# The first matrix of a single expert's block loaded and split amid the pair's block before it; the last pair block left whole

## The chip, the cores and the metric

The kernel runs on one core of one Trainium2 chip. The metric is device time in microseconds; before the change the median of three runs is 1378.51 us (1378.15 to 1379.26). The engines are PE (TensorE, matmuls), ACT (ScalarE), DVE (VectorE), POOL (GpSimd) and SP (SyncE, which issues nearly all loads here).

## The reference, cut to what matters

A decoder trunk of two layers over 256 positions of width 1024. The second layer ends in a mixture of experts: eight SwiGLU networks of hidden width 3584, of which each position uses two. What the change touches is this part alone:

```python
logits = (x2d @ router).astype(F32)
top_val, top_exp = lax.top_k(logits, TOP_K)          # 2 of 8
gates = jax.nn.softmax(top_val, axis=-1)
...
def expert_block(args):
    xb, e = args
    return (jax.nn.silu(xb @ w1[e]) * (xb @ w3[e])) @ w2[e]
```

All weights are fp32 and lie in HBM; the eight experts are 352 MB.

## The kernel before, in words

The kernel sorts the experts by how many positions chose them. The four fullest have room for 128 positions each and are computed one at a time, as **single** experts; the other four have room for 64 and are computed two at a time, as **pairs**: on PE the two experts of a pair use the two halves of the array's columns.

An expert's hidden width is cut into blocks of 512 columns, seven to an expert. A block is: the product with w1 (`up` or `up2`), silu of it on ACT (line 700), the product with w3, the gate product of both on DVE (line 711), four transposes of that (`gate_T`, lines 625 and 632), a copy or split of the transposed tile, and the product with w2 (`down`). The down products of a block are issued inside the following block, behind its w1 and silu. The blocks stand in a list `items` in the order single, single, pair; this **cycle** comes 14 times. In the kernel before, the last pair's last block is cut into two of 256 columns, so one more pair block follows at the end. At an expert's first block, `pre` gathers that expert's positions (lines 976 and 1001), and the down products of the block before are woven into that; in one block it first tests whether an expert has more positions than room (`overflow`, a branch that all engines take; line 888).

Single experts use a split: each weight tile comes from HBM as fp32 and is turned into hi (ACT, line 222, rounded to fp32r) and lo (DVE, line 223, what is left). `mm3` then makes three fp32r matmuls for each tile (lines 232 to 234). A block's w1 is two loads of 1 MB (`pieces`), four splits (p1 to p4) and 24 matmuls. The hi and lo tiles have five buffers each. Pair experts use fp32 directly: no split, four loads of 1 MB for each matrix (two halves of the rows, two experts), and 16 matmuls for each, which the trace records as two each (line 285 in `up2`, line 651 in `down`), so 32.

All these loads go through SP's queue in the order of the code, into 11 tiles of 1 MB in rotation; a load waits until the tile eleven loads before it has been read. In a cycle these are 24 loads.

The order of the instructions on each engine is not written out: the Tile framework plans it when the program is built. Its planner goes through the program with its own estimate of durations and gives each engine, of the instructions that it then holds ready, the one that stands first in the code. On the chip each engine keeps that order. So an instruction may be planned ahead of an earlier one that the planner believed to be waiting, and it stays there even where the chip would have had the earlier one ready.

In `swiglu` a block runs so: `step(u, 2)` issues the first half of w1's products, then `gate_T` of the block before, then `end(u)` the rest, then silu, `down` of the block before, then w3. In the list's last block (`held`) the down of the block before comes behind w3 instead. `tail=sums` starts the final sums (line 874) between the last down products.

Of the kernel before, what the change touches and what calls it, by code (L numbers as in the profile page):

```python
# [28 lines left out]
D_FFE = 3584  # L29
# [123 lines left out]
def trunk(ctx: ExitStack, tc: tile.TileContext, a, out, R=6, WB=5, NF=16):  # L153
# [60 lines left out]
    def load(w, r0, nr, c0, ncol):  # L214
        t = raw()
        v = t[:, :nr * ncol].rearrange("p (k f) -> p k f", k=nr)
        src = w.at(r0, nr, c0, ncol)
        nc.sync.dma_start(v if len(src.shape) == 3 else t[:, :nr * ncol], src)
        return v
# [16 lines left out]
    def pieces(w, c0, ncol, n, m=4):  # L236

        for r in range(0, KT, m):
            v = load(w, r, m, c0, ncol)
            for q in range(0, m, n):  # L240
                yield (r + q, *split(v[:, q:q + n, :]))
# [19 lines left out]
            sh, sl = s(k + j)  # L261
            mm3(o[:, :n], sh, sl, wh[:, j, :], wl[:, j, :], k + j == 0, k + j == KT - 1)

    def up(outs, w, c0, ncol, sta, ws=None, between=None):


        if ws is None:
            for q in pieces(w, c0, ncol, 2):
                for o, s in zip(outs, sta):
                    products(o, s, *q)  # L270
                yield
        else:
            for i in range(len(sta)):
                for q in ws:
                    products(outs[i], sta[i], *q)
                if i == 0 and between:
                    between()

    def up2(o, ws, c0, ncol, sta):

        for r in (0, 4):
            vs = [load(w, r, 4, c0, ncol) for w in ws]
            for k in range(4):
                for i, v in enumerate(vs):
                    TE.matmul(o[i * 64:(i + 1) * 64, :ncol], lhsT=sta(r + k, i), rhs=v[:, k, :], start=r + k == 0,  # L285
                              stop=r + k == KT - 1)
                if k % 2:
                    yield
# [175 lines left out]
    sta = halves(xTh, xTl)  # L464
# [126 lines left out]
    w1, w3, w2 = W["even_w1"][0], W["even_w3"][0], W["even_w2"][0]  # L591
# [9 lines left out]
    ws = ahead(w1, *chunks[0])  # L601
# [14 lines left out]
    def swiglu(items, ws, between=None, behind=None, next_ws=None, tail=None):  # L616

        def gate_T(it, g):  # L620
            n = it[4]
            if isinstance(it[0], tuple):
                pt, t = wk(), fa("gt")
                for j in range(n // P):
                    TE.transpose(pt[:, j * P:(j + 1) * P], g[0][:, j * P:(j + 1) * P], ident)
                A.copy(t[:, :n], pt[:, :n])  # L626
                return t
            gs = []
            for q in g:
                pt = wk()  # L630
                for j in range(n // P):
                    TE.transpose(pt[:, j * P:(j + 1) * P], q[:, j * P:(j + 1) * P], ident)  # L632
                gh, gl = fb("gh"), fb("gl")
                A.activation(gh[:, :n], pt[:, :n], AF.Copy)
                V.tensor_sub(gl[:, :n], pt[:, :n], gh[:, :n].bitcast(F32))  # L635
                gs.append((gh, gl))
            return gs

        def down(it, gs, fill=iter(())):
            w1, w3, w2, c0, n, sta, accs, first, last, pre, post = it  # L640
            nr = n // P
            accs = accs()
            if isinstance(w1, tuple):
                m = 1 if tail and it is items[-1] else 2
                for r in range(0, nr, m):
                    ws = [load(w, c0 // P + r, m, 0, D) for w in w2]
                    for j in range(m):
                        for d in range(2):
                            for i, w in enumerate(ws):
                                s = slice((r + j) * P + i * 64, (r + j) * P + (i + 1) * 64)  # L650
                                TE.matmul(accs[0][d][i * 64:(i + 1) * 64, :], lhsT=gs[:, s],  # L651
                                          rhs=w[:, j, d * 512:(d + 1) * 512], start=first and r + j == 0,
                                          stop=last and r + j == nr - 1)
                            step(fill)
                end(fill)
                if post:
                    post()
                return
            for r in range(0, nr, 2) if not last else [0]:
                ws = []  # L660
                m = 1 if tail and it is items[-1] else 2
                for q in range(r, nr if last else r + 2, m):
                    v = load(w2, c0 // P + q, m, 0, D)
                    ws += [split(v[:, j:j + 1, :]) for j in range(m)]
                for i, (gh, gl) in enumerate(gs):
                    for d in range(2):
                        for j, (wh, wl) in enumerate(ws):
                            s = slice((r + j) * P, (r + j + 1) * P)
                            c = slice(d * 512, (d + 1) * 512)
                            mm3(accs[i][d], gh[:, s], gl[:, s], wh[:, 0, c], wl[:, 0, c],  # L670
                                first and r + j == 0, last and r + j == nr - 1)
                            step(fill)
            end(fill)
            if post:
                post()

        prev = after = None
        for it in items:
            if it is items[-1] and next_ws:
                after = next_ws()  # L680
            w1, w3, w2, c0, n, sta, accs, first, last, pre, post = it
            fill = pre() if pre else None
            if fill:
                if prev:
                    step(fill, 3)
                    down(prev[0], gate_T(*prev), fill)
                    prev = None
                else:
                    end(fill)
            sta = sta()  # L690
            p1 = [wk() for _ in sta]
            two = isinstance(w1, tuple)
            u = up2(p1[0], w1, c0, n, sta[0]) if two else up(p1, w1, c0, n, sta, ws, between)
            step(u, 2)
            if prev:
                gs = gate_T(*prev)
            end(u)
            s = [fa("sl") for _ in sta]
            for q, p in zip(s, p1):
                A.activation(q[:, :n], p[:, :n], AF.Silu)  # L700
            held = tail and it is items[-1]
            if prev and not held:
                down(prev[0], gs)
            p3 = [wk() for _ in sta]
            with tc.issue_after(behind) if ws else nullcontext():
                end(up2(p3[0], w3, c0, n, sta[0]) if two else up(p3, w3, c0, n, sta))
            ws = None
            if held:
                down(prev[0], gs)
            for q, p in zip(s, p3):  # L710
                V.tensor_mul(q[:, :n], q[:, :n], p[:, :n])  # L711
            prev = (it, s)
        down(prev[0], gate_T(*prev), *([tail()] if tail else []))
        return after and after + next_ws(4)
# [5 lines left out]
    ws = swiglu([(w1, w3, w2, c0, n, lambda: sta, lambda: accs, i == 0, i == len(chunks) - 1, None, None)  # L720
            for i, (c0, n) in enumerate(chunks)], ws, rest, behind, lambda r=0: ahead(odd_in, 0, 512, r))
# [18 lines left out]
    p1 = proj(1)  # L740
# [4 lines left out]
    w1, w3, w2 = (W[q] for q in ("odd_w1", "odd_w3", "odd_w2"))  # L745
    ws = ahead(w1[0], 0, 512)
# [81 lines left out]
    with tc.issue_after(behind):  # L828
# [13 lines left out]
        for h in range(2):  # L842
# [8 lines left out]
            q = cp.tile([P, 8], F32, name=nm("slots"))  # L851
# [222 lines left out]
    def expert(q):  # L1074
        end_ = q == 6
        ch = [(c, 512) for c in range(0, D_FFE, 512)]
        if end_:
            ch[-1:] = [(D_FFE - 512, 256), (D_FFE - 256, 256)]
        ws3 = list(zip(picked(q), picked(q + 1))) if CAP[q] == 64 else picked(q)
        for i, (c, n) in enumerate(ch):  # L1080
            first, last = i == 0, i == len(ch) - 1
            pre = None
            if first:
                pre = lambda: begin([q])
            elif (q, i) == (0, 1):
                pre = residual
            elif (q, i) == (2, 2):
                pre = overflow
            yield (*ws3, c, n, lambda: state["sta", q], lambda: e_acc(q), first, last, pre,
                   (lambda: combine(q, end_)) if last else None)  # L1090

    alone, paired = run(*(expert(q) for q in range(4))), run(expert(4), expert(6))
    items = []
    for it in alone:
        items += [it, next(alone), next(paired)]
    items += paired
    swiglu(items, ws, behind=behind, tail=sums)


# [53 lines left out]
```

## Time and profile before

| | us |
|---|---|
| median of three runs | 1378.51 |
| lowest, highest | 1378.15, 1379.26 |
| the profiled execution | 1374.65 |
| its span, first to last instruction | 1372.9 |
| mean granted clock of TensorE | 0.982 |

| engine | busy, us | share |
|---|---|---|
| PE | 1301.1 | 95% |
| DVE | 784.9 | 57% |
| ACT | 614.4 | 45% |
| POOL | 53.7 | 4% |

The expert stage begins at about 460 us of the span and lasts to its end. Times in rows are microseconds from the start of the span. Matmuls are pipelined and the profiler models their ends, so a row of PE can overlap the next one by up to some tenths of a microsecond; starts are exact.

### The profile page before, as it was taken

Reading aid. Unit: us, or ns where it says so; the run is one execution under the profiler, and the core shown is the slowest. Engines: PE = TensorE matmul, PEld = TensorE weight load, DVE = VectorE, ACT = ScalarE, POOL = GpSimd, SP = SyncE. Lnnn points to the kernel's source line nnn. Section 1 sums busy time; section 2 is a strip of 40 time slices with the busy share of each in tenths; the row PEclk is TensorE's granted clock in tenths of the full one; section 3 lists DMA queues with packets and bytes.
Section 4 is the critical chain, followed back from the end, with each engine's and each line's share of the span. In section 5 each row is a group of like instructions: output and inputs, shape, how many; then the busy total and the mean of one; then the engine's idle time right before and its main releaser. Section 6 shows DMA issues by size and latency. Waiting matters only on the chain. (4 is left out here: it accounts for less than half of the span.)

```text
span 1372.9 us, 16689 instructions
## 1 busy us (share of the span) xinstructions
PE 1301.1 (95%) x6130; PEld 887.7 (65%) x6130; DVE 784.9 (57%) x1201; ACT 614.4 (45%) x859; POOL 53.7 (4%) x40
## 2 busy tenths in 40 slices
PE   8998999999999899999999999999899999999996
PEld 7776888887777775564746556466456475646562
DVE  6988445557777574463645455464446473644463
ACT  5564434443555364453444445254345353544441
POOL 0012000101021100000000000000000000000001
PEclk9999999999999699999999999999999999999998
DMA  9522456554444489999999999996999998999964
GB/s 371 193 101 103 166 184 218 221 194 162 155 151 176 170 308 396 422 420 421 412 375 421 419 420 409 381 362 226 420 421 412 405 411 344 421 415 418 394 234 167
DMA packets 69195, 426.26 MB, mean 310 GB/s; under 512 B 7920, under 2 KB 16368, under 8 KB 19824
## 3 DMA queue, kind: packets, MB, share of 16 engines
q1 hardware_dynamic: 68096, 421.70, 77.6%
q0 software_dynamic: 864, 3.15, 0.7%
q8 instruction: 50, 0.82, 0.2%
q14 instruction: 41, 0.34, 0.1%
q10 hardware_dynamic: 144, 0.26, 0.1%
HBM read 424.03 MB, written 1.05 MB: 310 GB/s over the span
## 5 line engine op out<-in xcount | busy, mean ns | idle before, releaser
L223 DVE TENSOR_TENSOR lo<-raw,hi 128x1024 fp32r<-128x1024 f32 (+1 forms) x454 | 535.2, 1220 | 244.1 <-ACT hi L222 237.3
L222 ACT ACTIVATE hi<-raw 128x1024 fp32r<-128x1024 f32 (+2 forms) x472 | 467.1, 1034 | 230.9 <-PE wk L234 124.2
L285 PE MATMUL wk<-raw,xg 128*64 128x512 f32 (+1 forms) x960 | 210.3, 568 | 0.2
L232 PE MATMUL wk<-hi,xg 128*128 128x512 f32 x448 | 179.3, 401 | 7.1 <-DVEq L888 6.6
L233 PE MATMUL wk<-lo,xg 128*128 128x512 f32 x448 | 178.4, 398 | 5.0 <-DVE lo L223 5.0
L234 PE MATMUL wk<-hi,xg 128*128 128x512 f32 x448 | 175.6, 392 | 0.0
L711 DVE TENSOR_TENSOR sl<-sl,wk 128x512 f32<-128x512 f32 (+1 forms) x55 | 36.4, 667 | 220.4 <-PE wk L285 132.4
L285 PEld LDWEIGHTS wk<-raw,xg 128*64 128x64 f32 x960 | 68.1, 137 | 120.9 <-issue 113.8
L232 PE MATMUL acc<-hi,gh 128*128 128x512 f32 x312 | 119.1, 401 | 15.1 <-ACT hi L222 14.5
L233 PE MATMUL acc<-lo,gh 128*128 128x512 f32 x312 | 123.3, 397 | 4.8 <-DVE lo L223 4.8
L234 PE MATMUL acc<-hi,gl 128*128 128x512 f32 x312 | 122.1, 394 | 1.4 <-DVE gl L635 1.2
L232 PEld LDWEIGHTS wk<-hi,xg 128*128 128x128 f32 x448 | 84.8, 189 | 43.9 <-issue 26.1
L233 PEld LDWEIGHTS wk<-lo,xg 128*128 128x128 f32 x448 | 84.9, 189 | 26.1 <-DVE lo L223 8.8
L651 PE MATMUL acc<-raw,gt 128*64 128x512 f32 x448 | 100.9, 598 | 0.3 <-ACT gt L626 0.3
L234 PEld LDWEIGHTS wk<-hi,xg 128*128 128x128 f32 x448 | 84.8, 189 | 17.0
L700 ACT ACTIVATE sl<-wk 128x512 f32<-128x512 f32 (+1 forms) x55 | 32.0, 582 | 137.1 <-PE wk L285 74.3
L232 PEld LDWEIGHTS acc<-hi,gh 128*128 128x128 f32 x312 | 58.3, 189 | 36.6 <-ACT hi L222 22.0
L233 PEld LDWEIGHTS acc<-lo,gh 128*128 128x128 f32 x312 | 59.1, 189 | 21.7 <-DVE lo L223 9.4
L232 PE MATMUL wk<-hi,xT 128*128 128x512 f32 (+1 forms) x192 | 72.6, 378 | 0.3 <-ACT xT L315 0.3
L233 PE MATMUL wk<-lo,xT 128*128 128x512 f32 (+1 forms) x192 | 71.7, 374 | 0.0
L234 PE MATMUL wk<-hi,xT 128*128 128x512 f32 (+1 forms) x192 | 71.6, 374 | 0.0
L651 PEld LDWEIGHTS acc<-raw,gt 128*64 128x64 f32 x448 | 35.2, 136 | 54.7 <-issue 54.0
(208 smaller groups left out, 1361.6 us busy)
## 6 DMA issues: line engine op xcount, KB each, us to landing
raw<-in_odd_w SPq DMA_DIRECT2D x326, 1024.0 KB, 9.7
raw<-in_even_w SPq DMA_DIRECT2D x31, 1024.0 KB, 4.8
raw<-in_odd_w_in SPq DMA_DIRECT2D x12, 1024.0 KB, 4.8
raw<-in_odd_w SPq DMA_DIRECT2D x20, 512.0 KB, 6.9
raw<-in_even_w_in SPq DMA_DIRECT2D x8, 1024.0 KB, 11.8
raw<-in_even_w_out SPq DMA_DIRECT2D x4, 1024.0 KB, 5.2
raw<-in_odd_w_out SPq DMA_DIRECT2D x4, 1024.0 KB, 5.5
raw<-in_even_w SPq DMA_DIRECT2D x4, 512.0 KB, 3.2
```

Of the source, the lines that this page charges most:

```text
L222: A.activation(hi, v, AF.Copy)
L223: by.tensor_sub(lo, v, hi.bitcast(F32))
L232: TE.matmul(o, lhsT=sh, rhs=wh, start=first, stop=False)
L233: TE.matmul(o, lhsT=sh, rhs=wl, start=False, stop=False)
L234: TE.matmul(o, lhsT=sl, rhs=wh, start=False, stop=last)
L285: TE.matmul(o[i * 64:(i + 1) * 64, :ncol], lhsT=sta(r + k, i), rhs=v[:, k, :], start=r + k == 0, stop=r + k == KT - 1)
L651: TE.matmul(accs[0][d][i * 64:(i + 1) * 64, :], lhsT=gs[:, s], rhs=w[:, j, d * 512:(d + 1) * 512], start=first and r + j == 0, stop=last a ...
L700: A.activation(q[:, :n], p[:, :n], AF.Silu)
L711: V.tensor_mul(q[:, :n], q[:, :n], p[:, :n])
```

## The change

`swiglu` now looks one block ahead. In a pair's block that is followed by a single expert's, it loads and splits the whole w1 of that next block (`list(pieces(...))`) behind the pair's down products and ahead of the pair's w3. The next block's `up` then takes these splits (`early`) instead of loading; its matmuls stay where they are in the code. And the last pair's last block is no longer cut in two, so it is the one that is `held`, and the load sizes of its down products change to two rows, one row, one row.

```diff
-    def up(outs, w, c0, ncol, sta, ws=None, between=None):
+    def up(outs, w, c0, ncol, sta, ws=None, between=None, early=None):
         if ws is None:
-            for q in pieces(w, c0, ncol, 2):
+            for q in early or pieces(w, c0, ncol, 2):
                 for o, s in zip(outs, sta):
                     products(o, s, *q)
                 yield
...
-                m = 1 if tail and it is items[-1] else 2
-                for r in range(0, nr, m):
+                for r, m in ((0, 2), (2, 1), (3, 1)) if tail and it is items[-1] else ((0, 2), (2, 2)):
                     ws = [load(w, c0 // P + r, m, 0, D) for w in w2]
...
-        prev = after = None
-        for it in items:
+        prev = after = early = None
+        for it, following in zip(items, items[1:] + [None]):
...
-            u = up2(p1[0], w1, c0, n, sta[0]) if two else up(p1, w1, c0, n, sta, ws, between)
+            u = up2(p1[0], w1, c0, n, sta[0]) if two else up(p1, w1, c0, n, sta, ws, between, early)
+            early = None
...
             if prev and not held:
                 down(prev[0], gs)
+            if two and following and not isinstance(following[0], tuple):
+                early = list(pieces(following[0], *following[3:5], 2))
             p3 = [wk() for _ in sta]
...
         ch = [(c, 512) for c in range(0, D_FFE, 512)]
-        if end_:
-            ch[-1:] = [(D_FFE - 512, 256), (D_FFE - 256, 256)]
...
     for it in alone:
         items += [it, next(alone), next(paired)]
-    items += paired
```

## Rows read from the trace of the kernel before

**Rows 1.** The page: busy us, share, count of PE; then DMA and GB/s by slice
```profile
PE 1301.1 (95%) x6130; PEld 887.7 (65%) x6130; DVE 784.9 (57%) x1201; ACT 614.4 (45%) x859; POOL 53.7 (4%) x40
...
DMA  9522456554444489999999999996999998999964
GB/s 371 193 101 103 166 184 218 221 194 162 155 151 176 170 308 396 422 420 421 412 375 421 419 420 409 381 362 226 420 421 412 405 411 344 421 415 418 394 234 167
```
**Rows 2.** Windows, one cycle: length, busy us by engine, clock, DMA share, GB/s
```profile
1008.82:1069.78 60.96, 57.94 (x253) 35.14 (x252) 30.97 (x29) 26.66 (x30) 0.00 (x0) 1.00 1.01 416
```
**Rows 3.** Timeline of PE, a pair's block: start, length, instructions, [idle before, releaser]
```profile
1258.22 1.07 PE L285 MATMUL wk<-raw,xg 128*64 128x512 f32 x2
1259.23 0.66 PE L632 MATMUL wk<-cst,sl 128*128 128x128 f32 x4
1259.81 7.08 PE L285 MATMUL wk<-raw,xg 128*64 128x512 f32 x30
1268.53 0.73 PE L232 MATMUL acc<-hi,gh 128*128 128x512 f32 x2 [1.63 <-ACT hi L222]
...
1275.04 7.09 PE L285 MATMUL wk<-raw,xg 128*64 128x512 f32 x32
...
1282.94 0.66 PE L625 MATMUL wk<-cst,sl 128*128 128x128 f32 x4 [0.38 <-DVE sl L711]
1284.08 0.50 PE L233 MATMUL wk<-lo,xg 128*128 128x512 f32 x1 [0.48 <-DVE lo L223]
...
1289.52 1.07 PE L651 MATMUL acc<-raw,gt 128*64 128x512 f32 x3
```
**Rows 4.** Timelines of DVE and ACT, the same stretch
```profile
1268.51 4.63 DVE L223 TENSOR_TENSOR lo<-raw,hi 128x1024 fp32r<-128x1024 f32 x4 [7.26 <-ACT hi L222]
1282.20 0.69 DVE L711 TENSOR_TENSOR sl<-sl,wk 128x512 f32<-128x512 f32 x1 [9.06 <-PE wk L285]
...
1267.42 5.79 ACT L222 ACTIVATE hi<-raw 128x1024 fp32r<-128x1024 f32 x6
```
**Rows 5.** Timeline of PE, the second pair's block
```profile
560.53 3.65 PE L285 MATMUL wk<-raw,xg 128*64 128x512 f32 x16
...
573.95 7.09 PE L285 MATMUL wk<-raw,xg 128*64 128x512 f32 x32
...
587.11 1.09 PE L651 MATMUL acc<-raw,gt 128*64 128x512 f32 x4
```
**Rows 6.** Waits from 520 us on: us in total, times, longest
```profile
PE acc L232 <- ACT hi L222: 14.5, 9, 1.6
...
PE wk L625 <- DVE sl L711: 4.1, 10, 0.6
```
**Rows 7.** Timeline of PE, the first of the two half blocks
```profile
1316.72 0.65 PE L285 MATMUL wk<-raw,xg 128*64 128x256 f32 x2
...
1322.48 1.95 PE L285 MATMUL wk<-raw,xg 128*64 128x256 f32 x16
```
**Rows 8.** Timeline of PE, a pair's w3 at a switch of experts
```profile
889.60 3.65 PE L285 MATMUL wk<-raw,xg 128*64 128x512 f32 x14
...
895.36 1.08 PE L651 MATMUL acc<-raw,gt 128*64 128x512 f32 x4 [0.28 <-ACT gt L626]
```
**Rows 9.** Timelines of PE and DVE behind the overflow test
```profile
970.75 0.77 PE L232 MATMUL wk<-hi,xg 128*128 128x512 f32 x1 [6.59 <-DVEq L888]
...
972.15 0.80 PE L233 MATMUL wk<-lo,xg 128*128 128x512 f32 x1 [0.21 <-DVE lo L223]
...
970.87 4.63 DVE L223 TENSOR_TENSOR lo<-raw,hi 128x1024 fp32r<-128x1024 f32 x4 [5.89 <-DVEq L888]
```
**Rows 10.** Windows, the end of the stage
```profile
1316.72:1358.82 42.10, 39.13 (x220) 21.39 (x219) 10.93 (x15) 7.16 (x11) 0.00 (x0) 1.00 0.59 209
```
**Rows 11.** Windows, a pair's w1 end to its w3, in two cycles
```profile
1204.45:1213.98 9.53, 7.37 (x25) 5.41 (x24) 4.63 (x4) 6.38 (x7) 0.00 (x0) 0.82 1.01 420
1266.82:1275.04 8.22, 6.06 (x26) 4.36 (x25) 4.63 (x4) 6.28 (x7) 0.00 (x0) 1.00 1.02 424
```

## The prediction

> **What bounds the kernel now.** I read the page first, then single cycles of the expert stage in the windows and the timelines. The page [rows 1] shows PE busy 95% of the span and the DMA engines at nine tenths or more in most slices of the second half; the reader is to see two candidates there, and that this view doesn't choose between them. One cycle (two single blocks, one pair block) chooses [rows 2]: 60.96 us, DMA share 1.01 at 416 GB/s, PE busy 57.94. Its weights are 24 loads of 1.049 MB, 25.2 MB, which at the 421 GB/s of saturated slices [rows 1] take 59.8 us. So the DMA engines have about 1.2 us to spare in a cycle. PE has 3.0 us of idle, and the timeline shows where: never behind a transfer. One wait of 1.63 us ends with a split on ScalarE, the other pair of waits (0.38 and 0.48 us) ends with VectorE [rows 3]. PE is the chain that sets the cycle; DMA stands close behind.
>
> The place of the change is the crossing from a pair's third-matrix products to the next single block. Today [rows 3]: w3 starts at 1275.04, then one single product, the wait, four transposes, the wait, 23 products, and the pair's down products start at 1289.52, which is 14.48 us. VectorE shows why [rows 4]: hi of the next matrix is long there (ScalarE made six in a row from 1267.42, of which four belong to the down weights), but its first lo stands behind the gate product L711, which waits for w3 until 1282.20. Where that lo stands ahead of L711, the crossing has no wait: 573.95 to 587.11, 13.16 us [rows 5]. So the wait costs 1.32 us. The transposes behind L711 waited on VectorE ten times [rows 6]; one of them is at the kernel's end, nine are crossings. The 1.63 us before the down products come nine times as well (one of them 1.45, at the end), and the change leaves them.
>
> **The change part by part.** *Moved.* In 13 pairs, two loads of the next single block's w1 go ahead of the pair's four w3 loads on SP, and four hi (1.0 us each on ScalarE) and four lo (1.2 us each on VectorE) ahead of L711. Nothing is added to POOL's queue. Those splits follow the down splits and are paced like them (4.63 us for four lo, against 1.3 us of products for each), so PE shouldn't wait for them. w3 lands about 5 us later (two loads of 2.5 us). I cost this at nothing: w3 P's products start far behind their landing now, since no wait of PE in [rows 3] ends with a DMA. If that lead were gone, each crossing would cost up to 5 us.
>
> *What goes, and what is late next.* With the lo's ahead of L711, the 1.32 us would go if PE's order stayed. But the order is made before the run, by a planner that takes the earliest instruction in the code among those that it holds ready. The trace shows what it believes: in the pair's w1 it issues one matmul (two records), then the gate's transposes, which the code puts behind all eight matmuls of that half, and then the rest [rows 3]; where it didn't expect a wait, 16 records stand together [rows 5]. It believes that the second expert's tile is still on its way. It also fills such waits across blocks: the first of the half blocks has one matmul alone at 1316.72, amid the single block's products [rows 7]. With w1 of the next block two loads ahead of w3 I expect it to put all 24 single products before w3, as they are ready while it waits for w3. On the chip w3 has landed, so nothing is gained there. And at w3's end nothing is left to cover gate product, transposes, copy: L711, L625, L626, and only then down. That chain has a row, at an expert's switch, where the fill beside it is short: PE's w3 ends at 893.25 (889.60+3.65), down starts at 895.36, 2.11 us [rows 8].
>
> The new crossing: 24 products x 0.235 us (from 1284.08 to 1289.52 are 23 of them, 5.44) = 5.6; w3 7.09; chain 2.11; sum 14.8 us, 0.3 more than now. If the planner also sends w3's first matmul alone among the single products, as it does at the head of w1, that one takes 1.01 us (1258.22 to 1259.23) and the other 30 records still take 7.08, so 15.8 us, 1.3 more. I take 1.3 for seven crossings, whose pair shows the lone first matmul today, and 0.3 for the two behind a gather, where 16 records stand together: 7 x 1.3 + 2 x 0.3 = 9.7. The early pairs have no wait now; if the order turns there too, 1.6 to 2.6 each. I take 1 for both, ends 0 and 5.
>
> *The block behind the overflow test.* PE starts one product at 970.75 and waits for lo until 972.15 (transposes between), since VectorE splits only from 970.87 [rows 9]. With splits done before the test this goes: -1.2 us (-0.5 to -1.5). At the switch to the third expert the matrix can't be used before its tokens are gathered: 0.
>
> *The last block whole.* Two pair blocks of 256 columns become one of 512. From the first half block's matmul (1316.72) to the end of the stage PE is busy 39.13 of 42.10 us, with the DMA share at 0.59 [rows 10]: PE and its waits set this part, not the loads, so their number there is priced at nothing. Work: four passes of 32 short records become two of 32 full ones; 16 short ones take 1.95 us [rows 7], so four passes 15.6, with lone starts about 16; two full ones 7.09 + 8.1 = 15.2. One silu wait of two goes. A wait between w3 and the single block's down of 1.3 us, as in the crossing, is likely to come, since down is now held behind w3. Waits now: 2.97 (42.10-39.13) and the parts that modelled ends hide; later about 1.3 to 2. I take -3 us (bounds -6 and +1).
>
> *Clock.* After one of these waits the granted clock was 0.82 in the stretch 1204.45 to 1213.98, which took 9.53 us where its fellows take 8.2 (1266.82 to 1275.04) [rows 3, 11]. The chain of 2.11 us has two such waits in each cycle; I put none into the sum and 0 to 4 us into the range. The Trainium skill (TensorE: Matmul & The Clock Gate, HAM oscillation) says that idle time between bursts of matmuls can send the clock to half; the row agrees for one wait in nine, so by it the new wait would speak against the change.
>
> Sum: 9.7 + 1 - 1.2 - 3 = +6.5 us. The profiled execution took 1374.65 us (span 1372.9, and 1.75 around it), 0.3% under the median 1378.51; the difference carries over: 1385.
>
> **Rivals.** *A, the order stays as the code has it* (single products behind w3). Then each crossing falls to 13.16, the DMA reserve of 1.2 us caps it: 9 x 1.2 = 10.8, with -1.2 and -3: -15, 1363.5. For it: the code's order, and the early pairs. Against it: the lone matmuls. It decides as soon as w3 is held landed when down ends. *B, single products first, but w3 unbroken*: 9 x 0.3 + 1 - 1.2 - 3 = -0.5, 1378. For it: the choice between 0.3 and 1.3 is a race of one landing against one lo in the planner. *C, the transfers bind.* DMA share 1.01 in [rows 2]: if they set the cycle, no order on PE matters, w1 and w3 only change places, and the tail alone moves: -4, 1374.5. Against it: no PE wait on a DMA, and 59.8 against 60.96. The Trainium skill (Perfetto Trace Analysis, Identifying the Most-Contended Engine) would have the most used resource improved, and DMA judged by its bandwidth; by that rule this is the case.
>
> **How the numbers follow.** My forecast 0.50 (its own range 1380 to 1392), A 0.24, B 0.17, C 0.09. About 0.2% (2.8 us) is what a measurement here can tell from no change. Forecast: slower but for a corner; A: faster; B: same; C: faster or same. Faster 0.29, same 0.20, slower 0.51. The range reaches from A's middle to the forecast's upper bound: 1363 to 1391.
>
> **What would show it.** In PE's timeline: single products between down and w3 at the crossings (A: behind w3); lone L285 pairs among them (B: none); L625 directly behind w3, with an idle stretch before it and before L651, about 2.1 us from w3's end to L651; a crossing of 15.8 us (B 14.8, A 13.2). Behind the overflow test no wait for lo. The stage's end: last L651 about 3 us earlier relative to the start of the last pair's w1. A wait of PE on a DMA at w3 would make the whole sum wrong; so would a cycle under 60.5 us.

## The result, and the profile after

The changed kernel takes 1393.53 us (median of 4 runs, 1389.51 to 1394.88) where the kernel before takes 1378.33 beside it: a ratio of 1.0106, 95% interval 1.0090 to 1.0122, so 15 us slower. The sign was forecast; the time lies above the forecast 1385.0 and 2.5 us outside the range.

The page after, and its costliest group on PE (out<-in, count, busy us, mean ns, idle before), answer to [rows 1]:

```profile
PE 1331.3 (96%) x6066; PEld 887.3 (64%) x6066; DVE 785.0 (56%) x1200; ACT 615.8 (44%) x857; POOL 53.7 (4%) x40
...
L285 PE MATMUL wk<-raw,xg 128*64 128x512 f32 x896 | 232.8, 598 | 0.1
```

PE is busy 30.2 us longer with 64 records fewer. L285 alone, the pairs' products of 64 columns for each expert, grew from 210.3 us (960 records) to 232.8: this is no new wait, it is slower work. The windows show the same for one cycle and for its crossing, the stretch from the start of the pair's w3 to its down products. They are to be held against 60.96 us in [rows 2] and 14.48 in [rows 3]:

```profile
1019.76:1082.20 62.44, 60.28 (x254) 35.07 (x253) 30.87 (x29) 26.65 (x30) 0.00 (x0) 1.00 0.99 408
1100.59:1116.51 15.92, 15.92 (x62) 7.06 (x61) 2.31 (x4) 0.62 (x2) 0.00 (x0) 1.00 0.98 402
```

In the crossing PE has no idle time at all, and the clock is at its upper level. The timeline of PE there shows what fills it:

```profile
1100.59 1.07 PE L285 MATMUL wk<-raw,xg 128*64 128x512 f32 x2
1101.59 0.50 PE L232 MATMUL wk<-hi,xg 128*128 128x512 f32 x1
...
1102.25 3.65 PE L285 MATMUL wk<-raw,xg 128*64 128x512 f32 x14
1105.83 0.50 PE L234 MATMUL wk<-hi,xg 128*128 128x512 f32 x1
...
1106.49 1.07 PE L285 MATMUL wk<-raw,xg 128*64 128x512 f32 x2
...
1109.98 2.37 PE L285 MATMUL wk<-raw,xg 128*64 128x512 f32 x10
...
1114.60 0.60 PE L625 MATMUL wk<-cst,sl 128*128 128x128 f32 x4
...
1116.51 1.94 PE L650 MATMUL acc<-raw,gt 128*64 128x512 f32 x8
```

Read it from start to start. w3 is cut into four pieces, with the next single block's products between them. A product of a pair leaves two records; the two experts' products stand next to each other, and in one piece 16 of them (32 records) take 7.09 us. Here the first stands alone and takes 1.00 (1100.59 to 1101.59, where the next product starts). The seven behind it (14 records) take 3.58 (1102.25 to 1105.83), as long as eight do in [rows 5], since one of the seven has no neighbour either. The same happens again in w3's second half. A product torn from its neighbour takes as long as two side by side; I call one such break a tear. With two tears w3 takes 9.16 us in place of 7.02. The single products and transposes between and behind its pieces take 6.76, against 6.14 where they stand together (in e3 below): each of the three further changes from pair products to single ones costs some 0.2. The transposes L625 are covered, with six products behind them. VectorE does all eight lo in a row, four of them the next matrix's, with the gate product (L713 now) behind:

```profile
1092.48 9.40 DVE L223 TENSOR_TENSOR lo<-raw,hi 128x1024 fp32r<-128x1024 f32 x8 [7.26 <-ACT hi L222]
```

The waits of PE (us in total, times, longest) answer to [rows 6]; the ten waits of the transposes behind the gate product are one (0.9 us, at the switch of experts), the eleven of up to 0.5 us for lo of an up product (5.0 us before) are gone, and eight of the nine waits behind hi stand:

```profile
PE acc L232 <- ACT hi L222: 13.0, 8, 1.6
...
PE acc L233 <- DVE lo L223: 5.5, 9, 1.3
...
PE wk L625 <- DVE sl L713: 0.9, 1, 0.9
```

Behind that hi wait stand the single block's 24 down products. In windows (the column behind the busy times is the granted clock) they now look like the slow stretch of [rows 11] more often than not. Of the two windows here the first stayed at the upper of its two levels (1.2 and 2.4 GHz), the second fell for a part of it:

```profile
760.05:766.24 6.19, 5.66 (x24) 4.34 (x24) 6.19 (x6) 6.19 (x7) 0.00 (x0) 1.00 1.02 424
1092.50:1100.30 7.80, 7.27 (x24) 5.51 (x24) 7.80 (x7) 6.48 (x7) 0.00 (x0) 0.78 1.00 415
```

Five of the eight stretches are slow in this execution, one in the profiled execution of before.

Behind the overflow test [rows 9] and at the end of the stage [rows 10], PE's timeline and one window:

```profile
982.51 0.77 PE L232 MATMUL wk<-hi,xg 128*128 128x512 f32 x1 [6.59 <-DVEq L890]
983.08 0.63 PE L233 MATMUL wk<-lo,xg 128*128 128x512 f32 x1
...
1356.20 0.73 PE L232 MATMUL acc<-hi,gh 128*128 128x512 f32 x2
1358.25 0.50 PE L233 MATMUL acc<-lo,gh 128*128 128x512 f32 x1 [1.32 <-DVE lo L223]
```

```profile
1340.73:1378.31 37.58, 35.85 (x145) 14.33 (x145) 10.51 (x14) 7.51 (x10) 0.00 (x0) 1.00 0.38 145
```

The wait for lo behind the test is gone. The last pair takes 37.58 us from its w1 on, where [rows 10] has 42.10 with eleven products of a single block (2.7 us) more in it: 1.8 us less.

The two profiled executions differ by 18.8 us of span. I add up the difference from the starts of PE's stages:

- Nine crossings cost 1.46 us more each (15.92 against 14.46), the early one without a wait [rows 5] 2.77, that at the switch of experts [rows 8] 1.07. Together 17.0.
- The lower clock costs 1.4 to 1.6 in each of four more blocks, 6.1.
- The block behind the test takes 0.8 less and the one before it 0.75 less, together -1.6.
- The end, from the last full crossing to the last down product, takes 2.0 less.
- At the switch the pair's down products take 1.15 longer and the single block behind them 1.1 less, which cancels.

That is 19.5 for 18.8; behind the last down product the changed kernel is 0.7 quicker. The profiled execution of before lies 3.7 us under the median beside it, that of the changed kernel at its median. If the clock makes that difference, only some 2.5 of its 6.1 us stand in the medians, by my estimate. The granted clocks of all executions fit: those of before run from 0.977 (1381.44 us, the slowest) to 0.984 and average 0.980 over 35, the four of the changed kernel average 0.9785, and the two profiled ones have 0.982 and 0.977.

### The profile page after: what moved, and what is told of

Read it like the earlier page. It is cut to its first block, busy times and chain, and to the rows that moved or that the text cites. A ratio compares the mean times of both kernels' runs of the same rounds, so it can differ in the third digit from the quotient of the medians.

```text
span 1391.7 us, 16543 instructions
## 1 busy us (share of the span) xinstructions
PE 1331.3 (96%) x6066; PEld 887.3 (64%) x6066; DVE 785.0 (56%) x1200; ACT 615.8 (44%) x857; POOL 53.7 (4%) x40
## 5 line engine op out<-in xcount | busy, mean ns | idle before, releaser
L285 PE MATMUL wk<-raw,xg 128*64 128x512 f32 x896 | 232.8, 598 | 0.1
L713 DVE TENSOR_TENSOR sl<-sl,wk 128x512 f32<-128x512 f32 (+1 forms) x54 | 36.2, 676 | 224.4 <-PE wk L285 139.2
L285 PEld LDWEIGHTS wk<-raw,xg 128*64 128x64 f32 x896 | 66.3, 136 | 127.8 <-issue 126.7
L234 PE MATMUL acc<-hi,gl 128*128 128x512 f32 x312 | 124.9, 402 | 0.2
L626 ACT COPY gt<-wk 128x512 f32<-128x512 f32 x14 | 8.2, 586 | 173.5 <-PE wk L625 173.5
```

The source lines that it names most:

```text
L234: TE.matmul(o, lhsT=sl, rhs=wh, start=False, stop=last)
```

## The experiments

Each time stands beside runs of the kernel before on the same chip.

**The end alone, and the early loads alone.** The first takes only what leaves the last block whole, the second undoes only that.

```diff
-        if end_:
-            ch[-1:] = [(D_FFE - 512, 256), (D_FFE - 256, 256)]
...
-    items += paired
```

> The kernel before with only the second part of the change: the last pair's last block whole, no load moved. Theory (the change loses by cutting up the pair's w3 matmuls, and gains at the end of the stage): the end gains the 2.0 us that the last pair is shorter in the trace after (66.72 against 68.71 us from the previous down products to the last), so 1376.3 us. Rival (the whole last block lengthens the chain behind the last matmul and is where the 15 us come from): 1380 to 1393.

> The kernel after with only the first part of the change: the last pair's last block is cut in two halves of 256 columns again. Theory: the whole loss sits in the early loads, so this one is 2 us slower than the kernel after: 1395.5 us. Rival (the end is what lost): 1380.

Measured: 1374.61 us against 1377.51, ratio 0.9977 (0.9967 to 0.9987); and 1398.34 against 1377.51, ratio 1.0142 (1.0125 to 1.0160). The end gains 2.9 us, and the early loads alone lose 20.8. The loss sits in the early loads; the rival of both falls. The second was expected at 1395.5 and is 2.8 us over it. Its clock may be a part of that: it averages 0.9765 where the changed kernel has 0.9785, with six slow stretches in the profiled execution instead of five.

**w3 kept together.** Nothing is taken from the change; the next single block's w1 products only get a place in TensorE's queue, behind the pair's last w3 product (`last2[0]`, noted in `up2`).

```diff
+            order = lambda: tc.issue_after(w3end) if w3end and not two else nullcontext()
+            with order():
+                step(u, 2)
...
+            with order():
+                end(u)
...
+            w3end = last2[0] if two else None
```

> The kernel after, loads and splits as early as there, but the next single block's w1 products are queued on TensorE behind the pair's last w3 matmul, so that w3's 64-column matmuls stay together. Theory (cut up w3): each crossing falls from 15.93 to 13.16 us, that of the trace before without its waits; 10 crossings by 2.77 us, 28 us, so 1366 us; if the half clock of five stretches was a matter of the same order, 5 us less still, 1361. Rival (the moved transfers cost it: w3's pieces land behind w1's): TensorE's order doesn't matter, w3 waits for its pieces and the time stays above 1385. My forecast's step (a gate chain left uncovered): falls as in the theory, since 24 products cover the chain again, by 2.1 us a crossing: 1372.

Measured: 1364.12 us, ratio 0.9895 (0.9878 to 0.9912): 29 us faster than the changed kernel, 13 faster than the one before. PE's timeline of the same crossing, then VectorE's:

```profile
1077.46 0.73 PE L232 MATMUL acc<-hi,gh 128*128 128x512 f32 x2 [1.63 <-ACT hi L222]
...
1085.53 7.09 PE L287 MATMUL wk<-raw,xg 128*64 128x512 f32 x32
...
1095.41 0.60 PE L627 MATMUL wk<-cst,sl 128*128 128x128 f32 x4
...
1098.69 1.51 PE L652 MATMUL acc<-raw,gt 128*64 128x512 f32 x6
```

```profile
1077.44 9.39 DVE L223 TENSOR_TENSOR lo<-raw,hi 128x1024 fp32r<-128x1024 f32 x8 [7.26 <-ACT hi L222]
1092.69 0.69 DVE L719 TENSOR_TENSOR sl<-sl,wk 128x512 f32<-128x512 f32 x1 [5.86 <-PE wk L287]
```

The crossing is 13.16 us (1085.53 to 1098.69), with the loads and splits as early as in the changed kernel and no PE wait for a transfer. Ten such crossings by 2.77 (15.93 against 13.16) are 27.7 of the 29 us. The transfers are no part of the loss, and the time is 8 us under the 1372 of an uncovered gate chain, my forecast's step. The half clock stayed (four of the eight stretches), so it isn't the cut-up w3 alone that brings it.

**The loads early, the splits not.** The pieces' loads are issued where the change has them, their hi and lo stand in the code behind the gate product again.

```diff
-                early = list(pieces(following[0], *following[3:5], 2))
+                vs = [(r, load(following[0], r, 4, *following[3:5])) for r in (0, 4)]
+                early = ((r + q, *split(v[:, q:q + 2, :])) for r, v in vs for q in (0, 2))
```

> The kernel after with only the loads of the next single block's w1 early; their splits (hi copies and lo subtractions) stand in the code where they stood before, behind the gate product. Theory (the planner already cuts up w3 for the earlier load; where the splits stand in the code is nothing): 1393.5 us, w3 in the same pieces. Rival (the early splits, which make the products ready while w3 runs, are what cuts it up): w3 in one piece and 1376.

Measured: 1394.29 us, ratio 1.0108 (1.0075 to 1.0141), the changed kernel's time. VectorE has its eight lo ahead of the gate product (L714 here) all the same, and PE cuts w3 in the same places (the first half of one w3):

```profile
1094.55 9.40 DVE L223 TENSOR_TENSOR lo<-raw,hi 128x1024 fp32r<-128x1024 f32 x8 [7.26 <-ACT hi L222]
1115.73 0.69 DVE L714 TENSOR_TENSOR sl<-sl,wk 128x512 f32<-128x512 f32 x1 [11.79 <-PE wk L285]
```

```profile
1102.64 1.07 PE L285 MATMUL wk<-raw,xg 128*64 128x512 f32 x2
...
1104.31 3.65 PE L285 MATMUL wk<-raw,xg 128*64 128x512 f32 x14
```

So the two moved loads suffice; the planner draws the rest from them. That it does so because it believes w3's pieces to be late is my reading; no run shows what it reckons with.

**The wait of the kernel before, without any load moved.** The load order is that of before and the last block is split. The next block's loads and splits are written behind w3, as they were, and the gate product is written behind them and queued on VectorE behind the second of the four lo.

```diff
+            if two and following and not isinstance(following[0], tuple):
+                early = list(pieces(following[0], *following[3:5], 2))
+            with tc.issue_after(los[-3]) if early else nullcontext():
+                for q, p in zip(s, p3):
+                    V.tensor_mul(q[:, :n], q[:, :n], p[:, :n])
```

> The kernel before with its order of loads and its split last block; the only thing that is made different is VectorE's queue: the pair's gate product (tensor_mul) stands behind the second lo subtraction of the next single block's w1 instead of ahead of the first. Theory: the waits of a crossing in the trace before (0.39 + 0.48 us and what lies around them, 14.46 against 13.16 us) come from that order alone, so 8 crossings by 1.3 us: 1368 us, and e3 differs from it by the end of the stage only (2 us less). Rival (the loads had to be moved for that): the lo's wait for their pieces, the gate product comes late, and it is at 1378 or above.

Measured: 1371.00 us, ratio 0.9947 (0.9935 to 0.9960), 6.5 us gained of the 10 expected. VectorE makes two more lo in the 9.06 us that it idled ahead of the gate product in [rows 4], and PE's timeline has a crossing of 13.16 us (1087.72 to 1100.88):

```profile
1079.64 6.90 DVE L225 TENSOR_TENSOR lo<-raw,hi 128x1024 fp32r<-128x1024 f32 x6 [7.26 <-ACT hi L224]
1094.88 0.69 DVE L717 TENSOR_TENSOR sl<-sl,wk 128x512 f32<-128x512 f32 x1 [8.35 <-PE wk L287]
```

```profile
1087.72 7.09 PE L287 MATMUL wk<-raw,xg 128*64 128x512 f32 x32
...
1100.88 3.66 PE L653 MATMUL acc<-raw,gt 128*64 128x512 f32 x16
```

The wait that the change set out from was an order of two instructions on VectorE, not a late load. From the starts of PE's stages, nine crossings are 1.3 us shorter each, 11.7 in all, and the switch is 1.1 longer. The rest is taken back by the lower clock: five of the eight stretches behind hi are slow in its profiled execution, and a sixth at the end, against one before, which costs some 8 us there. Over its six executions the clock averages 0.9765, over the 17 of before beside them 0.980.

**The wait behind hi, taken away.** ScalarE's silu of the pair stood ahead of the hi copies of w2 and waited 6.41 us for the pair's w1. The kernel before shows it, and the second wait that follows on PE:

```profile
1266.93 0.60 ACT L700 ACTIVATE sl<-wk 128x512 f32<-128x512 f32 x1 [6.41 <-PE wk L285]
1269.79 0.50 PE L233 MATMUL acc<-lo,gh 128*128 128x512 f32 x1 [0.53 <-DVE lo L223]
```

Now the silu is queued behind the hi copies. The first run does so in the changed kernel, the second in the one before.

```diff
+            late_ = two and prev and not held and not isinstance(prev[0][0], tuple)
+            if late_:
                 down(prev[0], gs)
...
+            with tc.issue_after(his[-1]) if late_ else nullcontext():
+                for q, p in zip(s, p1):
+                    A.activation(q[:, :n], p[:, :n], AF.Silu)
```

> The kernel after, but in a pair's block ScalarE's silu stands behind the four hi copies of the w2 that the single block's down products wait for, instead of ahead of them. In the trace after, that order makes TensorE wait 1.63 + 0.53 us in 8 pair blocks, and in 5 of them the 24 products behind the wait take 8.0 to 8.2 us instead of 6.56 (clock at its lower level). Theory (the half clock comes with this wait, whatever the order of w3): 8 x 2.16 = 17.3 us and some 8 us of clock, so 1369 us, and nothing left of the stretches of 8 us. Rival (the half clock follows the cut-up w3): 1376, the stretches stay long. Second rival (w2's pieces land only then): 1388 or above.

> The same edit of ScalarE's order in the kernel before, which has the same 8 waits of 1.63 + 0.53 us and w3 whole. By TensorE's sum alone: 1377.5 less 17.3 is 1360, and 1.5 us less for each stretch at the lower clock that goes. Rival (the transfers bind next): a cycle loads 24 MB, 25.2 million bytes, at the 421 GB/s which the trace of e3 shows in every slice, 59.8 us, and its cycles already last 59.6 to 59.8; the whole can't get under e3's stretch, and it is 1364 or above. Against e6 it tells what the cut-up w3 costs when the waits are gone: 13 us by my ledger of crossings, unless the transfers hide part of it.

Measured: 1367.16 us, ratio 0.9912 (0.9895 to 0.9928), and 1352.56, ratio 0.9815 (0.9801 to 0.9829), both against 1378.62. ScalarE's and PE's timelines of the first, and its PE waits:

```profile
1070.57 3.88 ACT L224 ACTIVATE hi<-raw 128x1024 fp32r<-128x1024 f32 x4
1077.09 0.60 ACT L707 ACTIVATE sl<-wk 128x512 f32<-128x512 f32 x1 [2.63 <-PE wk L287]
```

```profile
1068.38 1.07 PE L287 MATMUL wk<-raw,xg 128*64 128x512 f32 x2
...
1069.97 7.08 PE L287 MATMUL wk<-raw,xg 128*64 128x512 f32 x30
1076.98 0.73 PE L234 MATMUL acc<-hi,gh 128*128 128x512 f32 x2
```

```profile
PE wk L234 <- DVEq L896: 6.7, 1, 6.7
PE acc L235 <- DVE lo L225: 1.3, 1, 1.3
```

No hi wait is left, and all eight stretches take 5.76 us to the modelled end of their last product, in both runs, where with the wait they take 6.56, or 7.9 to 8.2 at the lower clock: the half clock comes with this wait. The wait costs more than the 2.16 us of idle time that I had priced: from the pair's 30 records to its w3 it is 15.23 us before (1259.81 to 1275.04) and 12.70 without it (1069.97 to 1082.67 in the first run). That is 2.5 us a block and 20 of the 26 us; the rest is the lower clock and, in the second run, 1.7 at the last pair. The Trainium skill (TensorE: Matmul & The Clock Gate, HAM oscillation) has idle time between bursts as what lowers the clock; these runs agree, though the idle here is only 1.63 and 0.53 us and doesn't always do it. The whole change costs 14.6 us between the two runs, with the wait behind hi gone from both; the sum above has 17.0 - 1.6 - 2.0 = 13.4 without the clock. My rival in the second run, a floor of 1364 us by the transfers, is refuted.

**All three edits, then one more.** The silu, the gate product and the whole last block, on the load order of before; and then the single block's gate transposes behind the first half of the pair's w1, so that no pair is torn there either.

```diff
+                with tc.issue_after(last2[0]) if two else nullcontext():
+                    gs = gate_T(*prev)
```

> The kernel before with three edits together: VectorE's gate product behind the second lo (e5), ScalarE's silu behind the four hi copies (e6), the last pair's last block whole (e1); no load moved. By TensorE's sum: e5's 1371.0 less 2.9 (e1) less 17.3, 1351, and 8 us less if the lower clock goes. By the transfers (59.8 us a cycle at 421 GB/s, which e3 already needs): no cycle gets shorter than e3's, 1361 to 1364.

> e7 with one edit more: the four gate transposes of a single block stand behind the first 16 of the pair's 32 w1 matmuls instead of behind the first two (which are the pair torn from its neighbours, 1.07 us for two records against 0.44 us each in a row). That prices a break of the 64-column matmuls by itself: 7 blocks by some 0.5 us on TensorE, 3.5 us less than e7 if TensorE binds; nothing if the transfers do.

Measured: 1338.69 us, ratio 0.9713 (0.9698 to 0.9727), and 1332.85, ratio 0.9669 (0.9654 to 0.9684). The first is 4 us under the lower end of TensorE's sum (1351, less 8) and 22 under the floor by the transfers. The second is the fastest of all, 46 us under the kernel before. PE's timeline and windows of it:

```profile
1167.06 3.65 PE L289 MATMUL wk<-raw,xg 128*64 128x512 f32 x16
1170.64 0.66 PE L636 MATMUL wk<-cst,sl 128*128 128x128 f32 x4
1171.23 3.65 PE L289 MATMUL wk<-raw,xg 128*64 128x512 f32 x16
1174.81 0.73 PE L234 MATMUL acc<-hi,gh 128*128 128x512 f32 x2
```

```profile
1167.06:1223.36 56.30, 56.30 (x255) 34.91 (x254) 31.03 (x29) 26.98 (x30) 0.00 (x0) 1.00 1.01 421
```

From w1 to the down products it is 7.75 us (1167.06 to 1174.81) where the torn one above takes 8.60 (1068.38 to 1076.98): 0.85 us is the price of one tear in w1, and the eight such blocks of e7 make 6.8, where 5.8 were measured (6.7 between the spans of the two profiled executions). I had expected 0.5 in seven. The cycle is 56.30 us, under the 59.8 that its 25.2 MB need at 421 GB/s, and PE is never idle. A cycle can outrun the transfers because they run ahead. SyncE's waits from 520 us on, of the kernel before and then of this one, show the lead being used: time in which a load stood waiting for its buffer shrinks, and waits for earlier loads to land take its place, while no wait of PE on a transfer comes up.

```profile
SPq L218 <- DVE lo L223: 299.3, 122, 5.3
SPq L218 <- PE wk L285: 217.2, 71, 10.3
SPq L218 <- PE acc L651: 104.3, 26, 8.9
```

```profile
SPq L218 <- PE wk L289: 202.7, 52, 10.3
SPq L218 <- DVE lo L225: 194.8, 90, 5.6
SPq L218 <- PE acc L654: 102.7, 27, 8.9
SPq L218 <- DMA raw<-in_odd_w: 86.3, 57, 2.4
```

That doesn't make the transfers free. The page of this run has 410 GB/s or more in 20 of the 22 slices from 565 us on to the last but one, so over the whole stage little of them is left to outrun:

```profile
GB/s 370 210 98 96 158 189 215 201 201 176 163 122 197 189 261 336 399 421 420 421 410 421 421 420 421 420 421 394 331 413 418 421 421 416 421 420 421 420 421 122
```

**The loads early, with the good orders.** e3 with the silu behind the hi copies.

> e3 (loads and splits early, w1's products held behind the pair's last w3 matmul, last block whole) with ScalarE's silu behind the four hi copies. It has e7's order on TensorE with the loads and splits moved, so it prices these by themselves. Theory (they cost nothing once w3 is whole): within 2 us of e7's 1338.7. Rival (w3's pieces land later and something waits): 4 us or more above it.

Measured: 1337.88 us, ratio 0.9702 (0.9689 to 0.9715), the same as e7 (0.9698 to 0.9727). Moving the loads and splits costs nothing and gives nothing, once PE's order is right.

## Why the prediction was right and wrong

*The cause.* The forecast was slower because the planner would put the next block's products ahead of w3 with one product torn off. The mechanism held: the loss is products of 64 columns without their neighbours (e3, e8, e7c). The order did not: "all 24 single products before w3" is the step that failed. Only 14 go between w3's pieces, in three places, and 10 are left behind it. That step sized the crossings at 10.7 us, and they measure 17.0. The other error of size is the clock, put at 0 where I estimate 2.5. With both the sum is 6.5 + 6.3 + 2.5 = 15.3, where 15.2 were measured.

*The crossing.* Two things were wrong in the forecast 15.8 us and cancelled. The chain of 2.11 us was priced as uncovered; with ten products left it is covered and costs 0. One tear was priced, at 1.0; there are two, at 2.14, and PE changes between the two kinds of products more often, 0.6. That 15.92 came out so near is luck. It holds for all nine crossings, not seven: the two behind a gather have their w1 in one piece as I read it, but w3 is cut there as elsewhere. The early pair costs 2.77 (forecast 1 with 5 as its end), the switch 1.07 (forecast 0). That makes 17.0 us where the sum had 10.7, the largest of the sum's errors.

*The clock.* I put 0 into the sum and let new waits price the range. No new wait came in the crossings; the old one behind hi was followed by the lower clock in five blocks instead of one. That is 6.1 us between the two profiled executions, and of the medians some 2.5 by the estimate above. Why it happens in some blocks and not in others is open: before and e1, which have the waits in the crossing as well, show it in one and two blocks, the kernels without these (after, e2, e3, e5, e8) in four to six. It is more than the chance of the profiled executions: over all executions the clock of the whole span averages 0.980 in before and in e1, and 0.9765 to 0.9785 in each of the other five. No run shows what links the two.

*The block behind the test* (-1.2) and *the last block whole* (-3) came out: -0.8, or -1.6 with the block before it, and -2.9 in e1, with the wait of 1.32 us at the place that was forecast.

*The rivals.* A was priced at 1363.5, and e3, which forces A's order, is at 1364.1. But my cap by the transfers, 1.2 us a cycle, was wrong as a rule: a lead of loaded buffers lets cycles run under 59.8 us. A's price came near all the same, since 1.2 is close to the 1.3 us that a crossing's wait costs. C falls with that, and with e3. By the Trainium skill's rule (Perfetto Trace Analysis, Identifying the Most-Contended Engine), which judges DMA by its bandwidth, the transfers were what to improve, at 416 GB/s; e7c took 46 us off without touching them. B's order, single products first and w3 unbroken, wasn't tried.

*Two slips.* They changed nothing: the forecast's own range ends at 1392 and the stated one at 1391, and the 3.0 us of idle time in a cycle has one more wait than was named, of 0.53 us behind the 1.63.

*Written off.* That the change leaves them was said of the nine waits of 1.63 us. It was right of the change, but for the one at the end, and passed over the largest thing in the trace, with a second wait of 0.53 behind each: 26 us by one instruction's place on ScalarE.

## What to carry to other kernels

Look at what stands next to what on an engine, not only at its idle time: two products that share the array must stay neighbours, and a load moved in the code can part them through the planner's order. Before moving a load to end a wait, read the queue of the engine that releases it; twice here a ready split stood behind an instruction that waited for later work, and pinning that one order beat every move of data. A resource at a share of 1.01 is no floor for a single cycle as long as its buffers hold a lead; over a whole stage it still counts.

## What the runs showed of the hardware

A 64-column product torn from its neighbour costs 0.85 us in w1 (8.60 against 7.75 us) and about 1.0 in w3 (9.16 against 7.02 for two), as much as two products side by side take (7.02 us for eight such pairs, 0.88 each). The Trainium skill (TensorE: Matmul & The Clock Gate, Part 3: Packing small matmuls) says that products whose outputs lie in different column groups run at the same time; the rows agree, and add that one odd product out of place is enough to lose a slot. A wait of 1.63 and 0.53 us on PE was followed by the lower clock level for a part of the next 24 products (0.77 to 0.79 on average, 1.4 to 1.6 us lost) in one to six of eight blocks of a profiled execution, and in none of the five runs without it (e6, both; e7, e7b, e7c).
